# Low parts of the projection weights and of the down weights' later operands: from GpSimd to VectorE

## The chip, the cores and the metric

The kernel runs on one core of a Trainium2 chip. The metric is device time in microseconds (us) of one execution: TensorE multiplies matrices, VectorE, ScalarE and GpSimd work elementwise, SyncE issues most of the transfers between HBM and the on-chip memory (SBUF). In the profile's rows PE is TensorE, PEld its weight loads, DVE VectorE, ACT ScalarE, POOL GpSimd and SP SyncE; the queue names with a q behind are the engines' sequencers.

## What is computed

One layer of a hybrid encoder on 1024 prompt tokens and 8 x 16 sample tokens (1152 in all), width 1024, in float32:

```
proj = einsum("btd,de->bte", rmsnorm(x, norm1_w), w_in)       # columns for three head groups
ya = rglru(causal_conv(xa)) * gelu(ga)                        # group A
yb = ssd_mixer(z, causal_conv(xbc), dt)                       # group B, chunked state
yc = hgrn_mixer(q, fpre, ig, og)                              # group C, chunked state
x = x + einsum("bte,ed->btd", concat(ya, yb, yc), w_out)
h2 = rmsnorm(x, norm2_w)
ff = silu(h2 @ w_ffn_gate) * (h2 @ w_ffn_up)                  # width 2816
x = x + ff @ w_ffn_down
y = rmsnorm(x, final_norm_w)
```

The outputs are y for both groups of tokens and the new states of the three head groups.

## The kernel before

Every float32 operand of a large product is split in two parts: a high part (`hi`, rounded by ScalarE to the matmul's own format) and a low part (`lo` = operand - hi). `mm3` then makes three matmuls of a product: hi x hi, hi x lo, lo x hi (lines L144, L145, L146). The low part is one subtraction of two SBUF operands, in L164 for weights that `load_w` brings in and in L180 (`split`) for everything else. This subtraction is what the change is about.

`load_w` takes a weight block of 128x1024 (two of 128x1056): a transfer into `wr_*` (two buffers), ScalarE's high part `wh_*`, the low part `wl_*` (three buffers each). The name's first letter tells the use: f, q, t, xa, ga, b for the input projection, o for the output projection (`w_out`). A counter for each of the two kinds picks the engine: of the input projection every fourth goes to VectorE (constants `WV`, `WO`), of the output projection the first alone (`XV`, `XO`), and `w_out` gives VectorE four more of its third chunk through `eng`; the rest goes to GpSimd. So of 31 input blocks 24 and of 24 output blocks 19 are on GpSimd.

The down projection works in groups of four blocks of the hidden width with a Strassen-like scheme of seven products for a pair of 2x2 blocks. `prep_a` prepares the weights of a group, for each of four column pairs `mp`: a transfer into `wd` (or, every fourth time, into the row buffer `rrow`), a first split of three operands (128x768; on VectorE, for mp 3 on GpSimd), four additions on VectorE (L1107 to L1110) that form the later four operands in place, and a second split of these (128x1024), on GpSimd. `prep_b` does the like for the activations (`e`, L1096), the larger piece on VectorE, the smaller on GpSimd. `products` runs the seven products and adds each to one or two accumulators on VectorE (L1204); `residual` adds the stored x on GpSimd (L1239, L1241). `prep_a` of the next group runs while the present one is multiplied.

Three more places matter. `proj_vdt` multiplies the nine token tiles with the t0 weights into two pairs of PSUM banks (`ptv`) and evicts them in L428 and L430 (`dtr`, `vs`); beside it `proj_f` makes 18 scans of 128x128 on VectorE (L410, `bc`), two tiles `ct` before them (L405) and two products on GpSimd (L406), and q1's tile is evicted in L311. `mix_c` prepares the C mixer's decay factors `W`: two subtractions on VectorE (L488, L489), an exponential (L490), products on VectorE and GpSimd (L498, L502), then the matmul `pat`. `mixt` loads the mixed rows through GpSimd's own queue.

The order of each engine's instructions is set when the program is built, by a list scheduler that works with modelled durations; each engine then executes in order. If an instruction changes engine, other instructions' places change too.

Of the kernel before, what the change touches and what calls it, by code (L numbers as in the profile page):

```python
# [51 lines left out]
WV = 4  # L52
# [12 lines left out]
WO = 0  # L65
XV = 100
XO = 1
# [23 lines left out]
def hybrid_step(ctx, tc, xT, xTp, vec, rows, nrow, wch, wtk0, wtk1, wout, wgate, wup, wdown,  # L91
# [3 lines left out]
    V, S, G, T = nc.vector, nc.scalar, nc.gpsimd, nc.tensor  # L95
# [52 lines left out]
    def feed():  # L148
        return tc.high_priority(offset=PRI)

    wcount, pcount, bcount = [0, 0], [0, 0], [0]

    def load_w(src, n, name, raw=None, ahead=True, eng=None):
        if raw is None:
            raw = wp.tile([P, 1056], F32, tag="wraw", name=f"wr_{name}", bufs=2)
        hi = wp.tile([P, 1056], F32R, tag="whi", name=f"wh_{name}")
        lo = wp.tile([P, 1056], F32R, tag="wlo", name=f"wl_{name}")
        with feed() if ahead else nullcontext():
            dma(raw[:, 0:n], src)
            S.activation(hi[:, 0:n], raw[:, 0:n], AF.Copy)  # L160
            o = name[0] == "o"
            wcount[o] += 1
            e = V if wcount[o] % (WV, XV)[o] == (WO, XO)[o] else G
            (eng or e).tensor_tensor(lo[:, 0:n], raw[:, 0:n], hi[:, 0:n].bitcast(F32), ALU.subtract)  # L164
        return hi, lo

# [11 lines left out]
    def split(dst_hi, dst_lo, src, eng):  # L178
        S.activation(dst_hi, src, AF.Copy)  # L179
        eng.tensor_tensor(dst_lo, src, dst_hi.bitcast(F32), ALU.subtract)  # L180
# [80 lines left out]
    def ch_tile(m, name):  # L261
        w = load_w(wch[m], 1024, name)
        for c in range(NCHUNK):
            hT = st["hT", c]
            tg = "a"
            if name[0] in "fq":
                tg = "aabbccc"[pcount[0] % 7]
                pcount[0] += 1
            pm = bank(tg, f"pm{name}_{c}", [CH])
            for k in range(KD):  # L270
                mm3(pm, wk(w, k, P), (hT[:, 0, k, :], hT[:, 1, k, :]), k == 0, k == KD - 1)
            yield c, pm
# [149 lines left out]
    def proj_vdt():  # L422
        w = [load_w(wtk0[h], 1056, f"t0{h}") for h in range(2)]
        for t, pm in tok_piece(w, 264, "v"):
            r = rstd1[:, t:t + 1]
            sg = pr.tile([P, 256], F32, tag="stg", name=f"vs{t}", bufs=2)
            with feed():
                V.scalar_tensor_tensor(dtr[:, t * 8:t * 8 + 8], pm[:, 0:8], r, dtb, ALU.mult, ALU.add)  # L428
                if VE:
                    V.tensor_scalar(sg, pm[:, 8:264], r, None, ALU.mult)  # L430
                else:
                    S.activation(sg, pm[:, 8:264], AF.Copy, scale=r)
                dma(vod[t, :, 0:256], sg)
# [12 lines left out]
    def proj_og():  # L446
        w = [load_w(wtk1[2, h], 1024, f"t3{h}") for h in range(2)]
        proj_gate(w, "og", vod[:, :, 256:512])
# [610 lines left out]
    def a_view(mp):  # L1059

        return AS[mp].rearrange("p (a f o s) -> p a f o s", a=2, f=2, s=P)
# [13 lines left out]
    def stage(n, name):  # L1075
        k = pcount[1] % 4
        pcount[1] += 1
        if k == 3 and n <= NTOK:
            return rrow[:, 0:n]
        if k == 1:  # L1080
            return pg.tile([P, 1280], F32, tag="xb", name=name)[:, 0:n]
        return io.tile([P, 1280], F32, tag="xTin", name=name, bufs=XB)[:, 0:n]
# [16 lines left out]
    def prep_a(g, mp):  # L1099
        t = stage(1024, f"wd{g}_{mp}")  # L1100
        v = a_view(mp)
        with feed():
            dma(t, wdown[mp, :, (2 * g - 1) * 512:(2 * g + 1) * 512])
            t = t.rearrange("p (f q s) -> p f q s", q=4, s=P)
            split(v[:, 0, :, 0:3], v[:, 1, :, 0:3], t[:, :, 0:3], G if mp in PA else V)

            V.tensor_tensor(t[:, :, 2], t[:, :, 3], t[:, :, 2], ALU.add)  # L1107
            V.tensor_tensor(t[:, :, 3], t[:, :, 0], t[:, :, 3], ALU.subtract)
            V.tensor_tensor(t[:, :, 0], t[:, :, 2], t[:, :, 0], ALU.subtract)
            V.tensor_tensor(t[:, :, 1], t[:, :, 1], t[:, :, 0], ALU.subtract)  # L1110
            split(v[:, 0, :, 3:7], v[:, 1, :, 3:7], t, G)


    acc = {}
# [174 lines left out]
    for g in range(NG):  # L1289
        final = g == NG - 1  # L1290
        for s in (1, 0):
            for mp in range(4):
                if g == 0:
                    products0(s, mp)
                    if s == 1:
                        prep_a(1, mp)
                    continue
                if final and s == 0:
                    products(g, s, mp, late)
                    for t in MID.split('/')[mp]:  # L1300
                        tokens_out(int(t))
                    continue
                products(g, s, mp)
                if not final and s == 0:
                    prep_a(g + 1, mp)
            if 0 < g < NG - 1:
                residual(s, g - 1)
            if not final:
                prep_b(g + 1, s)
# [86 lines left out]
```

## Time and profile before

| what | value |
|---|---|
| median of 3 runs | 1501.31 us (1500.36 to 1501.39) |
| the profiled execution's own time | 1499.57 us |
| its span, first to last instruction | 1497.8 us |
| TensorE busy | 1367.8 us (91%) |
| VectorE busy | 1122.1 us (75%) |
| ScalarE busy | 513.9 us (34%) |
| GpSimd busy | 792.9 us (53%) |
| mean granted TensorE clock | 0.960 |

Busy time of VectorE counts the time that an instruction stands still after it has begun. The stages in order: input projection and C mixer until about 410 us, z columns until 460, B mixer and output projection until 660, gate and up projection until 1190, down projection until 1450, final norm. TensorE is busy without a break from 750 to 1190 us; the change touches nothing there.

### The profile page before, as it was taken

What the parts mean: (1) busy time and instruction counts of PE and PEld (TensorE: products, weight loads), DVE (VectorE), ACT (ScalarE), POOL (GpSimd) and SP (SyncE); (2) the same over time, 40 slices, a digit from 0 to 9 for tenths busy, and PEclk for the clock granted to TensorE, in tenths of its full rate; (3) what the DMA queues carried; (4) which work ended last, traced back from release to release, by engine and by line L of the source; (5) the groups of instructions that cost most, each with busy time, mean ns of one, the idle gap of its engine ahead of it and who ended that gap; (6) DMA issues with size and microseconds to landing.
All of it is one profiled execution on the core that took longest, in us unless ns stands there. A gap on an engine that the chain in (4) does not pass through costs nothing. (4 is left out here: it accounts for less than half of the span.)

```text
span 1497.8 us, 24592 instructions
## 1 busy us (share of the span) xinstructions
PE 1367.8 (91%) x9309; PEld 1315.9 (88%) x9309; DVE 1122.1 (75%) x2028; ACT 513.9 (34%) x839; POOL 792.9 (53%) x615
## 2 busy tenths in 40 slices
PE   7979988899997889878799999999999999988886
PEld 6979887799987778878699999999999989988876
DVE  8476799888758688599646675665666768989896
ACT  6413334333344134354322222232231443322322
POOL 5336487767345555433534554544555464475553
PEclk9989999899999899988899999999999999999988
DMA  7253221432366786841413222223322262543523
GB/s 249 75 173 102 71 68 50 104 96 75 100 224 238 225 285 208 273 167 37 150 55 112 100 96 99 70 84 113 112 98 99 85 218 85 171 149 92 172 64 127
DMA packets 103370, 193.67 MB, mean 129 GB/s; under 512 B 10380, under 2 KB 62676, under 8 KB 103124
## 3 DMA queue, kind: packets, MB, share of 16 engines
q1 hardware_dynamic: 98356, 184.24, 37.4%
q0 software_dynamic: 4896, 7.87, 1.9%
q8 instruction: 73, 1.20, 0.3%
q14 instruction: 45, 0.37, 0.1%
HBM read 136.83 MB, written 55.23 MB: 128 GB/s over the span
## 5 line engine op out<-in xcount | busy, mean ns | idle before, releaser
L144 PE MATMUL pd<-e,as 128*128 128x320 f32 (+1 forms) x560 | 170.2, 305 | 25.4 <-DVE ac_pt L1204 9.1
L145 PE MATMUL pd<-e,as 128*128 128x320 f32 (+1 forms) x560 | 166.4, 298 | 0.8 <-DVE e L1096 0.8
L146 PE MATMUL pd<-e,as 128*128 128x320 f32 (+1 forms) x560 | 163.3, 297 | 0.6 <-POOL as L180 0.6
L144 PEld LDWEIGHTS pd<-e,as 128*128 128x128 f32 x560 | 106.8, 191 | 32.1 <-DVE ac_pt L1204 9.4
L180 POOL TENSOR_TENSOR al_u<-wr_u,ah_u 128x1024 fp32r<-128x1024 f32 x30 | 72.1, 2404 | 118.4 <-ACT ah_u L179 118.4
L180 POOL TENSOR_TENSOR al_g<-wr_g,ah_g 128x1024 fp32r<-128x1024 f32 x30 | 72.3, 2412 | 88.6 <-ACT ah_g L179 88.0
L145 PEld LDWEIGHTS pd<-e,as 128*128 128x128 f32 x560 | 107.1, 191 | 1.2 <-DVE e L1096 1.1
L146 PEld LDWEIGHTS pd<-e,as 128*128 128x128 f32 x560 | 106.5, 192 | 0.9 <-POOL as L180 0.9
L1005 POOL TENSOR_TENSOR g<-g,pt_u 128x256 f32<-128x256 f32 (+1 forms) x80 | 77.3, 985 | 22.9 <-DVE pt_u L1004 16.1
L179 ACT ACTIVATE ah_g<-wr_g 128x1024 fp32r<-128x1024 f32 x30 | 31.7, 1060 | 146.6 <-PE pS_u L145 71.8
L144 PE MATMUL pw<-mT,wh_o 128*128 128x384 f32 x192 | 69.1, 363 | 11.4 <-DVE xr L785 5.5
L498 POOL TENSOR_TENSOR qbd<-W,qkb 64x128 f32<-64x128 f32 x60 | 51.7, 861 | 48.7 <-ACT W L490 16.0
L144 PE MATMUL pS_g<-b,ah_g 128*128 128x256 f32 (+1 forms) x240 | 71.3, 298 | 5.2 <-ACT ah_g L179 5.2
L146 PE MATMUL pA_g<-b,al_g 128*128 128x256 f32 (+1 forms) x240 | 71.2, 297 | 0.5 <-POOL al_g L180 0.5
L144 PE MATMUL pA_g<-b,ah_g 128*128 128x256 f32 (+1 forms) x240 | 71.4, 298 | 0.0
L145 PE MATMUL pA_g<-b,ah_g 128*128 128x256 f32 (+1 forms) x240 | 71.0, 296 | 0.0
L145 PE MATMUL pA_u<-b,ah_u 128*128 128x256 f32 (+1 forms) x240 | 71.0, 296 | 0.0
L145 PE MATMUL pS_g<-b,ah_g 128*128 128x256 f32 (+1 forms) x240 | 71.0, 296 | 0.0
L144 PE MATMUL pA_u<-b,ah_u 128*128 128x256 f32 (+1 forms) x240 | 70.9, 295 | 0.0
L146 PE MATMUL pA_u<-b,al_u 128*128 128x256 f32 (+1 forms) x240 | 70.8, 295 | 0.0
L144 PE MATMUL pS_u<-b,ah_u 128*128 128x256 f32 (+1 forms) x240 | 70.4, 295 | 0.0
L145 PE MATMUL pS_u<-b,ah_u 128*128 128x256 f32 (+1 forms) x240 | 70.3, 295 | 0.0
(722 smaller groups left out, 5118.2 us busy)
## 6 DMA issues: line engine op xcount, KB each, us to landing
wr_o<-in_dram SPq DMA_DIRECT2D x24, 512.0 KB, 5.3
wr_g<-in_dram SPq DMA_DIRECT2D x20, 512.0 KB, 3.5
wr_u<-in_dram SPq DMA_DIRECT2D x20, 512.0 KB, 3.6
wd<-in_dram SPq DMA_DIRECT2D x15, 512.0 KB, 3.7
wr_t<-in_dram SPq DMA_DIRECT2D x14, 512.0 KB, 3.8
fr<-ffd SPq DMA_DIRECT2D x11, 640.0 KB, 4.0
ffd<-g SPq DMA_DIRECT2D x10, 640.0 KB, 3.0
ffd<-g SPq DMA_DIRECT2D x10, 512.0 KB, 2.9
```

The source lines that it names most:

```text
L144: T.matmul(out, ah, bh, start=start, stop=False)
L145: T.matmul(out, ah, bl, start=False, stop=False)
L146: T.matmul(out, al, bh, start=False, stop=stop)
L179: S.activation(dst_hi, src, AF.Copy)
L180: eng.tensor_tensor(dst_lo, src, dst_hi.bitcast(F32), ALU.subtract)
L498: (V, G)[r].tensor_tensor(Q[rs, l - lg, :, r, :].rearrange("p j (b m) -> p j b m", m=m), W[rs, l - lg].rearrange("p j (b two m) -> p j b t ...
L1005: G.tensor_tensor(g, g, u, ALU.mult)
```

## The change

All subtractions of `load_w` for which no engine is given go to VectorE, and so does the second split of `prep_a`.

```diff
             o = name[0] == "o"
             wcount[o] += 1
-            e = V if wcount[o] % (WV, XV)[o] == (WO, XO)[o] else G
+            e = V
             (eng or e).tensor_tensor(lo[:, 0:n], raw[:, 0:n], hi[:, 0:n].bitcast(F32), ALU.subtract)
...
             V.tensor_tensor(t[:, :, 1], t[:, :, 1], t[:, :, 0], ALU.subtract)
-            split(v[:, 0, :, 3:7], v[:, 1, :, 3:7], t, G)
+            split(v[:, 0, :, 3:7], v[:, 1, :, 3:7], t, V)
```

On GpSimd, in the down projection, one `prep_a` of group 3 stood before like this (`as0` to `as3` are the operands of the four `mp`, `128x2x512` is a second split, `e` is from `prep_b`, `xr`, `rrow` and `ac` from `residual`):

```order
L1096 TENSOR_TENSOR e1_11655<-fr3114_12813,e1_11655 128x960
L180 TENSOR_TENSOR as0_11657<-rrow_87,as0_11657 128x2x512
L180 TENSOR_TENSOR as3_11660<-wd3_3_13074,as3_11660 128x2x384
L180 TENSOR_TENSOR as1_11658<-wd3_1_12940,as1_11658 128x2x512
L1239 TENSOR_TENSOR rrow_87<-rrow_87 128x256
L1241 TENSOR_TENSOR ac_g0_11685<-ac_g0_11685,rrow_87 128x256
```

The second splits have left it; only mp 3's first split stays.

On VectorE the same place of the changed kernel (`pd2_...` are the products of the group before, `ac_...` the accumulators):

```order
L1110 TENSOR_TENSOR rrow_87<-rrow_87 128x2x128
L1204 TENSOR_TENSOR ac_pt01_11688<-ac_pt01_11688,pd2_024_12983 128x256
L1204 TENSOR_TENSOR ac_pt02_11689<-ac_pt02_11689,pd2_022_12991 128x256
L1108 TENSOR_TENSOR wd3_1_12940<-wd3_1_12940 128x2x128
L1204 TENSOR_TENSOR ac_g1_11686<-ac_g1_11686,pd2_021_12999 128x256
L1204 TENSOR_TENSOR ac_pt10_11690<-ac_pt10_11690,pd2_030_13017 128x256
L1204 TENSOR_TENSOR ac_pt11_11691<-ac_pt11_11691,pd2_030_13017 128x256
L180 TENSOR_TENSOR as2_11659<-wd3_2_13007,as2_11659 128x2x384
L1109 TENSOR_TENSOR wd3_1_12940<-wd3_1_12940 128x2x128
L180 TENSOR_TENSOR as0_11657<-rrow_87,as0_11657 128x2x512
L1204 TENSOR_TENSOR ac_pt12_11692<-ac_pt12_11692,pd2_036_13034 128x256
```

The last split but one row is the moved one, of mp 0; it follows mp 0's last addition (the first row) with eight rows between, and accumulator additions stand behind it. Before, the same rows stood there without it.

On VectorE, around the t0 tiles in the first 100 us (- is the order before, + the change; `wl_t30` is a moved low part, `ptv_0` the first t0 tile):

```order
-L405 SCALAR_TENSOR_TENSOR ct1_548<-f1_311,ct1_548 128x1152
+L164 TENSOR_TENSOR wl_t30_953<-wr_t30_951,wh_t30_952 128x1024
+L428 SCALAR_TENSOR_TENSOR dtr_307<-ptv_0_690,rstd1_86,rw_93 128x8
+L430 TENSOR_SCALAR vs0_715<-ptv_0_690,rstd1_86 128x256
 L410 SCALAR_TENSOR_TENSOR bc0_558<-cm_91,ct0_547 128x128
 L410 SCALAR_TENSOR_TENSOR bc0_558<-cio_80,ct0_547 128x128 x8
+L405 SCALAR_TENSOR_TENSOR ct1_548<-f1_311,ct1_548 128x1152
+L428 SCALAR_TENSOR_TENSOR dtr_307<-ptv_2_748,rstd1_86,rw_93 128x8
 L410 SCALAR_TENSOR_TENSOR bc1_573<-cm_91,ct1_548 128x128
-L410 SCALAR_TENSOR_TENSOR bc1_573<-cio_80,ct1_548 128x128 x8
-L428 SCALAR_TENSOR_TENSOR dtr_307<-ptv_0_690,rstd1_86,rw_93 128x8
-L430 TENSOR_SCALAR vs0_715<-ptv_0_690,rstd1_86 128x256
```

The eviction of the first t0 tile stood behind all 18 scans and stands before them now, right behind the moved low part; the eviction of q1 (L311), next in either order, now comes after the tenth scan, ahead of the last eight.

## Rows read from the trace of the kernel before

**Rows 1.** Busy time by stretch: length, then PE, PEld, DVE, ACT, POOL, PEclk, DMA share
```profile
85.30:89.30 4.00, 3.94 (x18) 3.97 (x19) 2.80 (x5) 2.22 (x2) 0.04 (x1) 0.50 0.91 250
100.00:460.00 360.00, 334.10 (x2192) 311.38 (x2191) 291.66 (x613) 139.15 (x244) 224.56 (x229) 0.96 0.35 108
460.00:660.00 200.00, 173.49 (x961) 160.88 (x960) 156.44 (x249) 73.67 (x138) 107.06 (x77) 0.91 0.72 230
1250.00:1450.00 200.00, 176.59 (x1255) 170.53 (x1253) 183.77 (x328) 57.40 (x62) 118.04 (x78) 0.97 0.41 128
```
**Rows 2.** TensorE's groups, 1190 to 1450 us: busy us, mean ns, idle before, releasers
```profile
L144 PE MATMUL pd<-e,as 128*128 128x320 f32 (+1 forms) x496 | 150.9, 306 | 24.4 <-DVE ac_pt L1204 9.1 <-DVE ac_whi L1204 6.9 <-DVE ac_g L1204 3.0
```
**Rows 3.** One line, L164: count, then shortest/median/longest in ns
```profile
L164 POOL TENSOR_TENSOR wl_o<-wr_o,wh_o x19: 2356/2387/3260, 484.2 to 646.0; 128x1024 fp32r<-128x1024 f32 x19
...
L164 DVE TENSOR_TENSOR wl_o<-wr_o,wh_o x5: 1212/1219/2810, 468.9 to 654.6; 128x1024 fp32r<-128x1024 f32 x5
```
**Rows 4.** Timeline of GpSimd, then VectorE, 1315 to 1324 us: start, length
```profile
1316.12 2.39 POOL L180 TENSOR_TENSOR as<-wd,as 128x1024 fp32r<-128x1024 f32 x1 [3.45 <-ACT as L179]
1318.47 0.92 POOL L1239 TENSOR_TENSOR rrow<-rrow 128x256 f32<-128x256 f32 x1
1319.35 2.48 POOL L1241 TENSOR_TENSOR ac_g<-ac_g,rrow 128x256 f32<-128x256 f32 x3
1321.79 2.58 POOL L180 TENSOR_TENSOR as<-wd,as 128x1024 fp32r<-128x1024 f32 x1
...
1315.54 0.41 DVE L1108 TENSOR_TENSOR wd<-wd 128x256 f32<-128x256 f32 x1
...
1316.67 2.13 DVE L1109 TENSOR_TENSOR wd<-wd 128x256 f32<-128x256 f32 x1
1318.72 0.95 DVE L1107 TENSOR_TENSOR wd<-wd 128x256 f32<-128x256 f32 x1
...
1321.26 0.85 DVE L1108 TENSOR_TENSOR wd<-wd 128x256 f32<-128x256 f32 x1
...
1322.83 1.83 DVE L1109 TENSOR_TENSOR wd<-wd 128x256 f32<-128x256 f32 x1
```
**Rows 5.** VectorE's groups, 1190 to 1450 us, shapes kept apart
```profile
L1096 DVE TENSOR_TENSOR e<-fr,e 128x1024 fp32r<-128x1024 f32 x10 | 19.4, 1949 | 7.0 <-ACT e L1093 7.0
L1109 DVE TENSOR_TENSOR wd<-wd 128x256 f32<-128x256 f32 x15 | 18.2, 1213 | 0.0
...
L180 DVE TENSOR_TENSOR as<-wd,as 128x768 fp32r<-128x768 f32 x9 | 14.0, 1560 | 1.6 <-ACT as L179 1.6
L1108 DVE TENSOR_TENSOR wd<-wd 128x256 f32<-128x256 f32 x15 | 11.8, 786 | 0.0
...
L1107 DVE TENSOR_TENSOR wd<-wd 128x256 f32<-128x256 f32 x15 | 9.3, 623 | 0.0
L180 DVE TENSOR_TENSOR as<-rrow,as 128x768 fp32r<-128x768 f32 x4 | 8.3, 2063 | 0.9 <-ACT as L179 0.9
```
**Rows 6.** Whom TensorE waited for: us in total, times, longest
```profile
PE pat L139 <- POOL W L502: 10.3, 6, 4.5
PE ptv L144 <- DVE vs L430: 9.6, 1, 9.6
```
**Rows 7.** Timeline of GpSimd, then VectorE, at 264 us
```profile
264.67 2.46 POOL L164 TENSOR_TENSOR wl_b<-wr_b,wh_b 128x1024 fp32r<-128x1024 f32 x1
...
264.57 0.28 DVE L488 TENSOR_TENSOR W<-qkb 128x128 f32<-128x128 f32 x1
264.77 2.50 DVE L489 TENSOR_TENSOR W<-qkb 128x128 f32<-128x128 f32 x1
```
**Rows 8.** Timeline of GpSimd, then VectorE, 74 to 85 us
```profile
74.53 2.48 POOL L164 TENSOR_TENSOR wl_t<-wr_t,wh_t 128x1024 fp32r<-128x1024 f32 x1
...
74.77 7.10 DVE L410 TENSOR_TENSOR_SCAN bc<-cio,ct 128x128 f32<-128x128 f32 x8
...
84.75 0.47 DVE L430 TENSOR_SCALAR vs<-ptv,rstd 128x256 f32<-128x256 f32 x1
```

## The prediction

> **What bounds the kernel now.** I read the busy shares by stretch first. From 100 to 460 us VectorE is busy 291.66 of 360 us and GpSimd 224.56; from 460 to 660 us it is 156.44 of 200 against 107.06; in the down projection, from 1250 to 1450 us, 183.77 of 200 [rows 1]. The first two stretches hold the moved low parts of `load_w`, the third those of `prep_a`. What the reader is to see: in the third VectorE leaves 16 us of 200 unused, so there it sets the pace beside TensorE. The grouped lines say the same from the other side: TensorE's first matmul of a product stood idle 24.4 us in the down stretch, and the releasers named first are VectorE's accumulator additions [rows 2]. Then I read one line, L164, for the price of the same instruction on either engine: median 2387 ns on GpSimd, 1219 ns on VectorE [rows 3].
>
> The view that decides most is the timeline of both engines together. While a GpSimd split of 2.39 us runs from 1316.12, a VectorE addition that begins at 1316.67 takes 2.13 us, and its like beside it takes 0.41 [rows 4]. VectorE's instructions with two SBUF operands stand still while GpSimd's runs. So a split on GpSimd isn't free for VectorE, and the question is whether it costs VectorE more from outside than from inside.
>
> **The change, part by part.** 63 instructions of 128x1024 change engine: 43 in `load_w` (24 of the input projection, 19 of the output projection) and 20 in `prep_a`. GpSimd loses some 63 x 2.4 = 151 us, VectorE gains 63 x 1.22 = 77 us [rows 3].
>
> *Down stage, 20 splits.* Added: 20 x 1.22 = 24.4 us. Taken away: what the old splits make VectorE wait. Lines L1107 to L1109 took 9.3 + 11.8 + 18.2 = 39.3 us for 45 instructions; unhindered 45 x 0.41 = 18.5, so 20.8 us is waiting, and 20/15 of it, 27.8, with the five groups that go through the row buffer [rows 4, 5]. The first splits (9 and 4 of 128x768) took 22.3 us against 13 x 0.92 = 12.0 (0.92 is an estimate, 768/1024 of 1.22), another 10.3. Together 38.1 us. Not all is due to the moved splits: of four late additions in the stretch shown, two wait for a moved split (1.72 + 1.42 us), two for residual work that stays (0.54 + 0.44), so I take 3.14/4.12 = 76%, 29.0 us. The new splits can themselves be held up by what GpSimd keeps: the nearest row is VectorE's other 128x1024 split, mean 1.95 us, 0.73 over its price, but it stands beside GpSimd's half of the same data, which the moved ones don't; I take 0.2 each, 4 us, between 0 and 14.6. Sum: 24.4 + 4 - 29.0 = -0.6, say **-1 us**. Ends: all 38.1 relieved and no new waiting, -13.7; half relieved and full new waiting, 24.4 + 14.6 - 19.0 = +20. VectorE executes in order, so behind each moved split stand accumulator additions, and TensorE waits for those; the order above shows them. The splits' wait for ScalarE's high part was harmless on GpSimd; the order puts eight VectorE rows between the last addition and the split, which I take to be enough for the high part.
>
> *Stretches 100 to 660 us, 38 splits.* Added 38 x 1.22 = 46.4 us. Relief per split as in the down stage, 29.0/20 = 1.45 us, times the lower share that VectorE is busy (448.1/560 = 80% against 92%): 1.26, so 48 us. VectorE's time is unchanged: **0**, between -6 and +6 for where the pieces fall in the order. GpSimd's relief, though, is clear gain where TensorE waits for it: 10.3 us for GpSimd's product with W in the C mixer [rows 6]. Ahead of one such wait a moved split from 264.67 turned a 0.28 us subtraction into 2.50 [rows 7]; the two large waits of this kind aren't both behind a moved split, so I take **-1.5 us**, between 0 and -6. Past GpSimd's queue, the loads of `mixt` are issued no later than before; I cost that at nothing, since the splits ahead of them only go away.
>
> *First 100 us, 5 splits.* The order around the t0 tiles changes. TensorE stood 9.6 us at 75 to 85 us for VectorE's eviction vs [rows 6], because that stood behind 18 scans, eight of which took 7.10 us beside GpSimd's work, a moved split from 74.53 among it [rows 8]. Afterwards the granted clock was 0.50, the lower level of 1.2 GHz, for some 4 us, which costs 2 more [rows 1]. In the new order the first eviction stands before the scans. The next thing late is the eviction of the q1 tile behind the first nine scans (some 3 us of waiting), then the C mixer's first loads, whose operands come from those scans. Of 11.6 us, 3.3 come back at once and more later; ends 0 and -11.6, I take **-5 us**.
>
> Sum: -5 - 1.5 + 0 - 1 = -7.5. The profiled execution took 1499.57 us, 1.74 below the median 1501.31, so I forecast 1492.1 in its terms and **1494 us** as a median.
>
> The Trainium skill's page SBUF — State Buffer, section Who interferes with whom, has a rule that speaks against the change: a VectorE instruction with two SBUF inputs and a GpSimd one that reads SBUF exclude each other, and whichever starts first keeps the port for its whole length. The trace agrees on one side (2.13 us for 0.41 above). By that rule each moved split would also stop GpSimd for up to 1.22 us; where GpSimd is the one waited for that could return the -1.5 us, which lies inside the bound given.
>
> **The rivals.** *No measurable change* (1498 to 1504). The waiting only changes sides: less behind GpSimd, as much on VectorE, and the early 5 us are eaten by the C mixer's chain. For it: VectorE's sums for 58 of the splits (24.4 + 4 + 46.4 = 75 added, 29 + 48 = 77 relieved) nearly cancel. Against: the 9.6 us gap has a visible cause that the new order removes. Time: 1501.3 - 1.5 = 1500. The Trainium skill's page Perfetto Trace Analysis, section Optimizing Scalar/DVE Operations, says of the shared port that moving work between these two engines might not help; that is this rival, and no row of the kernel before tells it from the forecast.
>
> *Slower.* Place: the down projection, where VectorE is 92% busy. If the relief per split falls below its price of 1.22 us, thus under 24.4 of the 38.1 us, VectorE's surplus delays the evictions and TensorE stops for banks. With half the relief and 0.4 us new waiting each: 24.4 + 8 - 19 = +13; less 5 early: 1501.3 + 8 = 1509; the bigger end, +20, would give 1516. For it: in-order VectorE, the idle row of TensorE. Against: the late additions stand right beside the moved splits in time.
>
> *Large gain* (1481 to 1486): the whole early gap and clock, 10, and two thirds of the down stage's -13.7. Against: several other waits follow each.
>
> That the change doesn't do what it says can be put aside: the order shows the 63 instructions on VectorE.
>
> **How the numbers follow.** About 0.2%, 3 us, is what a measurement can tell from no change. Forecast and large gain together 0.50 (0.44 and 0.06), no change 0.22, slower 0.28. The likeliest case alone reaches from 1484 to 1498, by halving and doubling its terms. Since both signs hold much, the range takes in the slower rival: 1481 to 1513, which leaves out some 0.15 to 0.2, the far bounds.
>
> **What would show it.** VectorE's busy time near 1122 us although it has 63 instructions more, GpSimd's near 640. L1107 to L1109 near 0.5 us each. The moved splits at 1.2 to 1.4 us. No 9.6 us wait of ptv, TensorE done with the t0 tiles some 5 us sooner. The down stage of the same length within 3 us. I am wrong if ptv's gap stays or reappears as a wait of the C mixer, if the splits take 2 us and more on VectorE, or if TensorE's idle time before pd grows beyond 24.4 us.

## The result and the profile after

The changed kernel takes **1459.61 us** (median of 4 runs, 1456.95 to 1461.40) against 1500.84 for the kernel before on the same chip: ratio 0.9725, 95% interval 0.9708 to 0.9742. That is 41 us less. I had forecast 1494, with a range from 1481 to 1513: the sign was right, the size far off, and the time lies outside the range.

The page of the changed kernel, busy time and clock over the span of 1455.2 us:

```profile
PE 1354.3 (93%) x9309; PEld 1309.0 (90%) x9309; DVE 1098.5 (75%) x2091; ACT 515.3 (35%) x839; POOL 641.4 (44%) x552
```

GpSimd lost 151.5 us and 63 instructions, as forecast. VectorE has those 63 more and is busy for 23.6 us *less* (1122.1 before); I had expected no difference. The moved instruction has the forecast price, to be set against [rows 3]:

```profile
L164 DVE TENSOR_TENSOR wl_o<-wr_o,wh_o x24: 1209/1225/3312, 450.5 to 633.3; 128x1024 fp32r<-128x1024 f32 x24
L164 DVE TENSOR_TENSOR wl_t<-wr_t,wh_t x16: 1205/1224/1259, 51.0 to 445.6; 128x1024 fp32r<-128x1024 f32 x14, 128x1056 fp32r<-128x1056 f32 x2
```

**Where the time went.** A mark is the moment at which TensorE's first or last instruction of a tile begins or ends in the trace; the profiled execution of each kernel is compared with that of the kernel before:

| mark | before, us | after, us | gain so far |
|---|---|---|---|
| last `ptv` (t0 tiles) | 108.0 | 100.8 | 7.2 |
| last `ptog` | 135.4 | 132.0 | 3.4 |
| last `po` (C mixer) | 395.4 | 391.8 | 3.6 |
| first `ptz` (z columns) | 398.8 | 387.6 | 11.2 |
| last `ptz` | 482.0 | 470.6 | 11.4 |
| last `px` (B mixer) | 591.0 | 573.3 | 17.7 |
| last `pw` (output projection) | 666.1 | 644.9 | 21.2 |
| last `pA_u` (up projection) | 1188.0 | 1164.8 | 23.2 |
| first `pt` (final norm) | 1454.1 | 1410.1 | 44.0 |

So some 18 us come between 135 and 666 us, and 21 in the down projection, which takes 245 us in place of 266. The first `ptz` comes 11.2 us sooner because the z columns now begin before the C mixer's last products; at the end of these (`po`) TensorE is 3.6 us ahead, as at 135 us. The 18 us come behind the C mixer: 8 until the last z columns, 6 until the last `px`, 3.5 until the last `pw`. Busy time of the whole down stage, before and after (columns as in [rows 1]):

```profile
1188.00:1454.00 266.00, 239.20 (x1705) 231.87 (x1704) 233.81 (x415) 86.21 (x111) 153.90 (x98) 0.97 0.42 132
```
```profile
1165.00:1410.00 245.00, 234.43 (x1703) 228.64 (x1702) 221.76 (x434) 87.00 (x111) 101.32 (x78) 0.99 0.47 144
```

VectorE has 19 recorded instructions more and 12.0 us less to do. Before the first matmul of a product TensorE now stands 7.7 us, where it stood 25.4 on the page of before [rows 2], and its releasers have changed: ScalarE's and VectorE's parts of the weights, no longer the accumulators.

```profile
L144 PE MATMUL pd<-e,as 128*128 128x256 f32 (+1 forms) x560 | 167.2, 300 | 7.7 <-ACT as L179 4.6
L146 PE MATMUL pd<-e,as 128*128 128x256 f32 (+1 forms) x560 | 162.3, 297 | 3.1 <-DVE as L180 3.1
```

VectorE's groups in the same stage, to be set against [rows 5]: L1107 to L1109 fell from 623, 786 and 1213 ns to 567, 575 and 505, L1096 of 1024 columns from 1949 to 1324 (L1110 rose from 457 to 639), and the moved splits themselves cost 18.8 + 6.4 = 25.2 us.

```profile
L180 DVE TENSOR_TENSOR as<-wd,as 128x1024 fp32r<-128x1024 f32 x15 | 18.8, 1261 | 0.0
L1096 DVE TENSOR_TENSOR e<-fr,e 128x1280 fp32r<-128x1280 f32 x10 | 15.1, 1511 | 10.4 <-ACT e L1093 10.4
L1096 DVE TENSOR_TENSOR e<-fr,e 128x1024 fp32r<-128x1024 f32 x10 | 13.2, 1324 | 2.5 <-ACT e L1093 2.5
L180 DVE TENSOR_TENSOR as<-wd,as 128x768 fp32r<-128x768 f32 x11 | 12.2, 1111 | 2.3 <-ACT as L179 2.3
L1110 DVE TENSOR_TENSOR wd<-wd 128x256 f32<-128x256 f32 x15 | 9.6, 639 | 0.0
L1108 DVE TENSOR_TENSOR wd<-wd 128x256 f32<-128x256 f32 x15 | 8.6, 575 | 0.0
L1107 DVE TENSOR_TENSOR wd<-wd 128x256 f32<-128x256 f32 x15 | 8.5, 567 | 0.0
L1109 DVE TENSOR_TENSOR wd<-wd 128x256 f32<-128x256 f32 x15 | 7.6, 505 | 0.0
L180 DVE TENSOR_TENSOR as<-rrow,as 128x1024 fp32r<-128x1024 f32 x5 | 6.4, 1275 | 0.0
```

In the B mixer one line shows it best: L744, which scales the mixer's rows before they are transposed for the output projection. Before:

```profile
L744 DVE SCALAR_TENSOR_TENSOR ws<-ws,ssb,nwr 128x256 f32<-128x256 f32 x8 | 12.7, 1632 | 2.1 <-POOL ssb L172 2.1
L744 DVE SCALAR_TENSOR_TENSOR wb<-wb,ssb,nwr 128x256 f32<-128x256 f32 x10 | 10.6, 1095 | 0.8 <-POOL ssb L172 0.8
```

and after:

```profile
L744 DVE SCALAR_TENSOR_TENSOR wb<-wb,ssb,nwr 128x256 f32<-128x256 f32 x10 | 4.5, 479 | 0.7 <-POOL ssb L172 0.7
L744 DVE SCALAR_TENSOR_TENSOR ws<-ws,ssb,nwr 128x256 f32<-128x256 f32 x8 | 3.6, 482 | 0.9 <-POOL ssb L172 0.9
```

Of the 18, seven took 2.4 to 3.2 us before, and the other eleven 0.47 or 0.48. Beside each of the seven a 2.4 us subtraction of `load_w` on GpSimd was running. TensorE's transposes (`pmb`) stood for these rows before:

```profile
PE pmb L748 <- DVE ws L744: 4.0, 2, 2.5
PE pmb L748 <- DVE wb L744: 3.3, 2, 1.8
```

After, TensorE has no wait for L744. The timeline of one pair in the kernel before (GpSimd, VectorE: start, length), and of the same pair after:

```profile
577.18 2.40 POOL L164 TENSOR_TENSOR wl_o<-wr_o,wh_o 128x1024 fp32r<-128x1024 f32 x1
...
577.24 3.01 DVE L744 SCALAR_TENSOR_TENSOR wb<-wb,ssb,nwr 128x256 f32<-128x256 f32 x2 [0.82 <-POOL ssb L172]
```
```profile
562.11 0.88 DVE L744 SCALAR_TENSOR_TENSOR wb<-wb,ssb,nwr 128x256 f32<-128x256 f32 x2 [0.36 <-POOL ssb L172]
```

A second trail is in the waits of SP's queue, which issues the loads in a fixed order. In the down stage of the kernel before, the loads of the next activations (L1090) and of the stored x (L1237) stood for GpSimd's low parts, since these had to be done with a buffer before it could be filled again:

```profile
SPq L1090 <- POOL as L180: 53.5, 11, 9.5
SPq L1237 <- POOL as L180: 35.3, 4, 10.2
```

After, the first is 22.5 us behind VectorE's low parts, and the second is gone from the longest waits:

```profile
SPq L1090 <- DVE as L180: 22.5, 9, 7.0
SPq L1103 <- POOL e L1096: 21.8, 10, 2.8
SPq L1237 <- DVE ac_whi L1204: 14.3, 1, 14.3
```

These are waits of a queue that runs ahead, so they aren't time by themselves; but they are a way for a slow low part to cost time, beside the way through VectorE.

### The profile page after: what moved, and what is told of

Read it like the earlier page. It is cut to its first block, busy times and chain, and to the rows that moved or that the text cites. A ratio compares the mean times of both kernels' runs of the same rounds, so it can differ in the third digit from the quotient of the medians.

```text
span 1455.2 us, 24583 instructions
## 1 busy us (share of the span) xinstructions
PE 1354.3 (93%) x9309; PEld 1309.0 (90%) x9309; DVE 1098.5 (75%) x2091; ACT 515.3 (35%) x839; POOL 641.4 (44%) x552
## 4 chain that ended last, share of the span: by engine, by line
PE 60%; DVE 22%; DMA 8%; issue 4%; POOL 2%; ACT 2%; SPq 0%; DVEq 0%; POOLq 0%; ACTq 0%
PE pS_g L144 3%; PE pS_g L145 3%; PE pd L144 3%; PE pS_u L144 3%; PE pS_g L146 3%; PE pS_u L145 3%; PE pS_u L146 3%; PE pd L146 3%; PE pd L145 3%; PE pA_u L144 2%; PE pA_u L146 2%; PE pA_u L145 2%; PE pA_g L145 2%; PE pA_g L144 2%; PE pA_g L146 2%
## 5 line engine op out<-in xcount | busy, mean ns | idle before, releaser
L144 PE MATMUL pd<-e,as 128*128 128x256 f32 (+1 forms) x560 | 167.2, 300 | 7.7 <-ACT as L179 4.6
L146 PE MATMUL pd<-e,as 128*128 128x256 f32 (+1 forms) x560 | 162.3, 297 | 3.1 <-DVE as L180 3.1
L145 PE MATMUL pd<-e,as 128*128 128x256 f32 (+1 forms) x560 | 164.6, 295 | 0.0
L180 POOL TENSOR_TENSOR al_u<-wr_u,ah_u 128x1024 fp32r<-128x1024 f32 x30 | 72.1, 2403 | 119.0 <-ACT ah_u L179 116.1
L180 POOL TENSOR_TENSOR al_g<-wr_g,ah_g 128x1024 fp32r<-128x1024 f32 x30 | 71.9, 2397 | 90.4 <-ACT ah_g L179 89.6
L498 POOL TENSOR_TENSOR qbd<-W,qkb 64x128 f32<-64x128 f32 x60 | 54.3, 905 | 62.5 <-ACT W L490 25.6
L144 PE MATMUL pS_u<-b,ah_u 128*128 128x256 f32 (+1 forms) x240 | 70.6, 295 | 0.0
L146 PE MATMUL pS_u<-b,al_u 128*128 128x256 f32 (+1 forms) x240 | 70.5, 294 | 0.0
```

What stands on the lines that cost most here:

```text
L144: T.matmul(out, ah, bh, start=start, stop=False)
L145: T.matmul(out, ah, bl, start=False, stop=False)
L146: T.matmul(out, al, bh, start=False, stop=stop)
L498: (V, G)[r].tensor_tensor(Q[rs, l - lg, :, r, :].rearrange("p j (b m) -> p j b m", m=m), W[rs, l - lg].rearrange("p j (b two m) -> p j b t ...
```

## The experiments

Three theories. **A**: a GpSimd subtraction holds VectorE, and the gain is there where TensorE waits for VectorE. **B**: the scheduler's other order is what gained. **C**: GpSimd's time or queue is what costs, whoever waits. Later **D**: the low part is simply ready sooner. All ratios are against the kernel before.

**1 to 4: the parts.** Each keeps one part of the change. In the first, only `load_w`:

```diff
-            split(v[:, 0, :, 3:7], v[:, 1, :, 3:7], t, V)
+            split(v[:, 0, :, 3:7], v[:, 1, :, 3:7], t, G)
```

> The 43 low parts of load_w on VectorE, the 20 of prep_a on GpSimd as before. Theory A (a GpSimd subtraction holds VectorE, and what counts is where TensorE waits for VectorE): the changed kernel was 23 us ahead of the one before at the start of the down projection and 44 us ahead at its end, so this half alone gives about -21 us (1476 to 1484 us), all of it before 1190 us, and the down stage is as long as before (266 us). Theory B (the gain is the other order of instructions, not the moved work): the halves do not add up; this one and the other half together miss -41 us by over 8 us. Theory C (what counts is GpSimd time freed, whoever waits): 43 of 63 subtractions, so -28 us (1473 us).

In the second, only `prep_a`:

```diff
-            e = V
+            e = V if wcount[o] % (WV, XV)[o] == (WO, XO)[o] else G
```

> The 20 low parts of prep_a on VectorE, the 43 of load_w as before. Theory A: about -21 us (1476 to 1484 us), all of it between the start and the end of the down projection, which takes 245 us in place of 266. Theory B: not the rest of -41 us to e1_loadw_only, off by over 8 us. Theory C: 20 of 63, so -13 us (1488 us).

The third and fourth divide `load_w` (with `prep_a` on GpSimd): `e = V if not o or ...` for the input projection, `e = V if o or ...` for the output projection.

> Only the 24 low parts of the input projections on VectorE. Theory A: the gain before 500 us is where these weights are used (t0, t1 and the first of mixer B), so this takes most of what load_w gives: -14 to -21 us (1480 to 1487 us). Theory C: 24 of 63, so -16 us (1485 us). They are told apart by the next run, not by this one.

> Only the 19 low parts of the output projection on VectorE. Theory A: between 500 and 720 us the changed kernel gained nothing and at 745 us some 3 us, so -2 to -5 us (1496 to 1499 us). Theory C: 19 of 63, so -12 us (1489 us). Theory B: any figure, and with e3_input_only not the sum that e1_loadw_only shows.

The marks are those of the one profiled execution of each kernel; for `prep_a` only and for the input part it was 4 and 6 us faster than the median.

| kernel | median, us | ratio (95%) | last `px` | last `pw` | last `pA_u` | down stage |
|---|---|---|---|---|---|---|
| before | 1500.14 | | 591.0 | 666.1 | 1188.0 | 266 |
| load_w only | 1479.41 | 0.9847 (0.9827 to 0.9866) | 573.8 | 648.2 | 1169.3 | 265 |
| prep_a only | 1483.57 | 0.9881 (0.9852 to 0.9910) | 589.6 | 662.1 | 1185.9 | 248 |
| input only | 1495.32 | 0.9964 (0.9940 to 0.9988) | 587.2 | 658.1 | 1180.3 | 264 |
| output only | 1485.95 | 0.9896 (0.9878 to 0.9914) | 579.6 | 654.8 | 1175.1 | 265 |

The halves add up: 1.53% + 1.19% = 2.72%, against 2.75% for the whole; with intervals of 3 to 4 us on each half, so close a match is in part luck. The gain of each half lies in its own stage: `load_w` leaves the down stage at 265 us, `prep_a` shortens it to 248 and leaves the rest nearly as it was. B is unlikely as the main cause, since it would have to give two independent orders that happen to add up; that some us of each half come from the other order isn't excluded. C's figures (28 and 13 us) were missed too: measured 23 and 18.

My division of `load_w` was wrong. The output projection's 19 gave 15.6 us (I had expected 2 to 5) and the input projection's 24 gave 5.4 (expected 14 to 21). The trace tells why: the weights of the output projection are prepared ahead, beside the B mixer, and there they hold VectorE's small instructions, L744 among them, not those of the output projection. With the output part alone TensorE is level at the first `px` (421.0 in both) and 11.4 us ahead at the last. With the input part alone it is 10.6 us ahead at the first `px` (410.4) and only 3.8 at the last; with the other 19 moved too, the lead grows from 10.8 to 17.2.

**5 and 6: a useless GpSimd instruction in the down stage.** The changed kernel, with one line more behind `prep_a`'s split; the operand `t` isn't read after it:

```diff
+            G.tensor_tensor(t, t, v[:, 0, :, 3:7].bitcast(F32), ALU.subtract)
```

> The changed kernel, with a useless GpSimd subtraction of the same size (operand and high part read, the result written over the operand, which nobody reads again) behind each of prep_a's 20 VectorE subtractions. No low part comes later for it; GpSimd has its load of before, and its two reads. Theory A (a GpSimd subtraction holds VectorE): the down stage goes back from 245 towards 266 us, so 1472 to 1482 us in place of 1460. Theory D (what gained was that the low part is ready 1.2 us sooner, on VectorE): no change, 1457 to 1463 us.

or with two memsets of the same tile in its place:

```diff
+            for _ in range(2):
+                G.memset(t, 0.0)
```

> As e5_ghost_reads, but with two memsets of the operand in place of the subtraction: about 2 x 1.05 = 2.1 us of GpSimd each time (0.52 us for 512 columns in the trace of before), without a read. Theory A in its narrow form (it is GpSimd's reads that hold VectorE): 1458 to 1465 us. Theory C (GpSimd's queue or its load is what costs): the same as e5_ghost_reads, 1472 to 1482 us.

Measured: 1492.73 us (0.9951, 0.9934 to 0.9968) with the subtraction, 1471.48 (0.9814, 0.9793 to 0.9834) with the memsets. Against 0.9725 that is 34 and 13 us; the down stage takes 281 and 254 us in place of 245. A had allowed 12 to 22 and up to 5. C had forecast 1472 to 1482 us for both, and they lie 21 us apart. The low parts are made by VectorE in both, so D alone doesn't explain the gain. The down stage with the subtraction and with the memsets, to be set against the changed kernel's above:

```profile
1165.00:1446.00 281.00, 247.66 (x1701) 238.95 (x1700) 254.07 (x432) 87.61 (x112) 159.81 (x99) 0.95 0.40 125
```
```profile
1168.00:1422.00 254.00, 233.58 (x1694) 228.04 (x1693) 222.35 (x428) 86.72 (x111) 143.38 (x118) 0.99 0.44 139
```

With the subtraction TensorE stood 33 us in the stage where it had stood 11, and it was busy 13 us longer, at a granted clock of 0.95 in place of 0.99. VectorE's rows with the subtraction, beside GpSimd's; L1205 is the accumulator addition, one line lower than before:

```profile
L1112 POOL TENSOR_TENSOR wd<-wd,as 128x1024 f32<-128x1024 f32 x15 | 40.8, 2727 | 21.0 <-DVE as L180 21.0
...
L180 DVE TENSOR_TENSOR as<-wd,as 128x1024 fp32r<-128x1024 f32 (+1 forms) x26 | 38.8, 1500 | 3.9 <-ACT as L179 3.9
L1096 DVE TENSOR_TENSOR e<-fr,e 128x1280 fp32r<-128x1280 f32 (+1 forms) x20 | 34.2, 1713 | 14.5 <-ACT e L1093 14.5
L1205 DVE TENSOR_TENSOR ac_whi<-ac_whi,pd 128x320 f32<-128x320 f32 x62 | 27.3, 474 | 2.1 <-PE pd L146 2.0
L180 DVE TENSOR_TENSOR as<-rrow,as 128x1024 fp32r<-128x1024 f32 (+1 forms) x9 | 15.5, 1720 | 0.2 <-ACT as L179 0.2
```

and with the memsets:

```profile
L1113 POOL MEMSET wd<- 128x1024 f32 x30 | 28.4, 956 | 18.9 <-DVE as L180 18.4
...
L180 DVE TENSOR_TENSOR as<-wd,as 128x1024 fp32r<-128x1024 f32 (+1 forms) x26 | 34.4, 1325 | 4.8 <-ACT as L179 4.6
L1096 DVE TENSOR_TENSOR e<-fr,e 128x1280 fp32r<-128x1280 f32 (+1 forms) x20 | 30.3, 1514 | 20.5 <-ACT e L1093 20.5
```

Beside the subtraction VectorE's instructions with two SBUF operands (L180 from `wd`, and L1096, both forms together) grew from 1198 to 1500 and from 1418 to 1713 ns; the accumulator addition, one of whose operands lies in PSUM, stayed at 474. VectorE's busy time in the stage rose from 222 to 254 us, with the memsets only to 222.4. In the memset kernel the two means grew as well, to 1325 and 1514, but not beside the memsets: of the rows of L180, L1096 and L1107 to L1110, 21 ran beside a memset and no other GpSimd instruction, and each took what its like took beside none (128x256 additions 409 to 417 ns, 128x1024 subtractions 1209 to 1216). The long ones all ran beside a GpSimd instruction that reads SBUF. So GpSimd's subtraction holds VectorE and its writing doesn't, which is A in its narrow form. The 13 us that the memsets cost all the same are beyond A's range and just below C's. The added instructions also changed the order of the others (on VectorE at least 220 of 2091 stand elsewhere with the subtraction, 249 with the memsets), so neither time is that of the added work alone.

**7 and 8: the same behind `load_w`'s 43 subtractions**, on the raw weight:

```diff
+            if eng is None and wcount[o] % (WV, XV)[o] != (WO, XO)[o]:
+                G.tensor_tensor(raw[:, 0:n], raw[:, 0:n], hi[:, 0:n].bitcast(F32), ALU.subtract)
```

> The changed kernel, with the same useless GpSimd subtraction behind load_w's VectorE subtraction, for the 43 weights whose low part GpSimd made before. Theory A: most of load_w's 23 us comes back, above all between 410 and 650 us, so 1474 to 1485 us. Theory D: 1457 to 1464 us.

> As e7_ghost_loadw with two memsets of the raw weight, 2.1 us without a read. Theory A in its narrow form: 1458 to 1467 us. Theory C: the same as e7_ghost_loadw. A wait for the raw weight's buffer, which both hold some 2 us longer, would show in both.

Measured: 1516.45 us (1.0113, 1.0093 to 1.0133), slower than the kernel before, and 1482.53 (0.9887, 0.9858 to 0.9916) with memsets. Both are beyond what A allowed them, by 31 and 16 us, and in the same pattern: the memsets cost 23 us, and the subtraction 34 us more than that. TensorE was 51 us behind the changed kernel at the last `px` with the one, 14 with the other. With the memsets 12 us more were lost between the last `pw` and the last `pA_u`, behind the last of these weights; I didn't find why.

**9: more of the same.** If GpSimd's subtractions cost so much, nine more of them go to VectorE:

```diff
-PA = (3,)
+PA = ()
...
-            split(b_part(s, k, 0, 0, 3), b_part(s, k, 1, 0, 3), t[:, 0:3, :], (V, G)[k % 2])
+            split(b_part(s, k, 0, 0, 3), b_part(s, k, 1, 0, 3), t[:, 0:3, :], V)
```

> The changed kernel, with two more groups of GpSimd subtractions on VectorE: the first low part of each down weight whose mp is 3 (5 in all, 2.06 us on GpSimd in the trace after) and two of the four first low parts of each of build's two calls (4 in all, 2.2 to 2.4 us). Theory A: VectorE pays about 1 us for each and is held less; TensorE waits only 10.8 us in the down stage of the changed kernel, so -1 to -4 us in all (1455.5 to 1458.5 us). Rival: VectorE, at 222 of 245 us, is now what TensorE waits for, and each of the 9 costs about 1 us: +5 to +9 us (1465 to 1469 us).

Measured: 1465.79 us (0.9779, 0.9757 to 0.9801), 8 us slower than the changed kernel by the ratios. The time is the rival's: the down stage went from 245 to 252 us, where TensorE's waits for the accumulator additions grew from 2.5 to 7.5 us and those for ScalarE's high parts from 4.6 to 7.1, and the gate projection's first products ended 5 us later. VectorE's busy time in the stage hardly changed (222 and 223 us): what the moved subtractions added was about what was relieved.

**10, 14 and 15: the buffer, the order, or the reads.** A memset of 8 columns of the operand, which holds its buffer with next to no work for GpSimd; the same on a dead tile `n2`, meant as the same instruction without the buffer; and half the useless subtraction:

```diff
+            G.memset(t[:, 1, 3, 0:8], 0.0)
```

> The changed kernel with one GpSimd memset of 8 columns of the operand (0.1 us) behind each of prep_a's 20 VectorE subtractions. The operand's buffer is held until GpSimd has come to it, as in e5_ghost_reads and e6_ghost_writes, but GpSimd has next to no work for it. If the 12 us of e6_ghost_writes are the holding of the buffer and the turn in GpSimd's queue, this has most of them: 1466 to 1472 us. If they are GpSimd's 2 us of writing, or the other order of the instructions: 1458 to 1463 us.

```diff
+            G.memset(n2, 0.0)
```

> As e10_touch, but the 0.1 us memset goes to eight columns of a scale that nobody reads any more (n2), so that the operand's buffer is not held for it. If the 11 to 12 us of e10_touch and e6_ghost_writes are the holding of the buffer until GpSimd has come to it: 1458 to 1463 us. If any added instruction moves the others so that the time goes up: 1466 to 1472 us.

```diff
+            G.tensor_tensor(t[:, 1], t[:, 1], v[:, 0, 1, 3:7].bitcast(F32), ALU.subtract)
```

> As e5_ghost_reads, with half the columns (512 of 1024) in the useless GpSimd subtraction. The buffer is held as in e10_touch (1471 us). If each column that GpSimd reads holds VectorE, the time lies half way between e10_touch and e5_ghost_reads (1492 us): 1478 to 1486 us. If it is the instruction and not its reads: 1468 to 1474 us.

| written behind each of the 20 splits | median, us | ratio (95%) | down stage, us |
|---|---|---|---|
| nothing (the changed kernel) | 1459.61 | 0.9725 (0.9708 to 0.9742) | 245 |
| 8 columns of a dead tile (ran before the stage) | 1462.95 | 0.9760 (0.9739 to 0.9781) | 247 |
| 8 columns of the operand | 1470.98 | 0.9813 (0.9790 to 0.9837) | 259 |
| two memsets of the operand | 1471.48 | 0.9814 (0.9793 to 0.9834) | 254 |
| half the subtraction | 1475.10 | 0.9844 (0.9827 to 0.9860) | 260 |
| the whole subtraction | 1492.73 | 0.9951 (0.9934 to 0.9968) | 281 |

The kernel with the dead tile isn't the comparison that I meant it to be. Nothing ties its memsets to the splits, and the scheduler put all 20 far ahead of the stage; those on the operand ran behind their splits (first and last start in us):

```profile
L1112 POOL MEMSET vc<- x20: 94/104/137, 662.8 to 668.2; 128x8 f32 x20
...
L1112 POOL MEMSET wd<- x15: 95/104/112, 1181.2 to 1417.3; 128x8 f32 x15
```

All its other instructions stand in the order of the changed kernel, on every engine. So its 5 us by the ratios, 2 in the down stage, are no price of another order: they show how far two measurements of the same order can lie apart. (Of the 7.9 us between the two profiled executions 5.3 had been lost at the last `pw`, before the first memset.)

The 8 columns of the operand cost 13 us, by the ratios and in the down stage alike. They hold the buffer until GpSimd has come by, and they changed the order as well: on VectorE at least 59 of 2091 instructions stand elsewhere. How much is the one and how much the other isn't shown. That two memsets of the whole operand cost no more speaks against the time that GpSimd works. In the trace of the 8 columns SP's queue stands for GpSimd again:

```profile
SPq L1090 <- POOL wd L1112: 22.4, 10, 5.1
...
SPq L1238 <- POOL rrow L1112: 13.8, 2, 9.2
SPq L1238 <- POOL wd L1112: 13.2, 4, 8.7
```

The half subtraction cost 5 us more than the touch by the ratios, 1 in the down stage of the profiled executions, and so lies between my two ranges, where I had put 10; the whole one cost 21. The cost isn't in proportion to what GpSimd reads. VectorE is busy 230.6, 235.2 and 254.1 us in the three. The stage with the half subtraction, to be set against that with the whole one above:

```profile
1165.00:1424.00 259.00, 237.74 (x1702) 229.07 (x1701) 235.17 (x430) 88.41 (x112) 131.58 (x98) 0.99 0.44 137
```

Of the 22 us between them 10 are TensorE's busy time, at a granted clock of 0.99 and 0.95, and 12 its idle time. Why the second half brings so much more waiting I didn't settle.

**11 and 12: the C mixer.** There GpSimd's product of keys and weights (L502) is what TensorE waits for longest in the changed kernel, and GpSimd reads there 120 times beside VectorE:

```diff
-                G.tensor_tensor(w0, w0, halves(kk, m)[0], ALU.mult)
+                V.tensor_tensor(w0, w0, halves(kk, m)[0], ALU.mult)
```

> The changed kernel, with the C mixer's 60 products of keys and weights (L502, 865 ns each on GpSimd) on VectorE, where the neighbouring products of 128x128 (L488, L489) take 0.30 to 0.39 us: VectorE pays 15 to 20 us between 100 and 410 us, where it is busy 250 of 310 us. Theory A: VectorE is held less by GpSimd's reads (its excess over its shortest durations is 40 us there), and TensorE's 8.4 us of waiting for L502 go: -3 to -8 us (1452 to 1457 us). Rival: VectorE is the engine that TensorE waits for there, and pays more than it is relieved: 0 to +8 us (1460 to 1468 us).

> As e11_keys_on_vector, and the 60 products of queries that GpSimd makes (L498, 905 ns) on VectorE too (412 ns there): GpSimd reads nothing in that loop any more. Theory A: VectorE pays 15 us more than in e11_keys_on_vector (60 x 0.25 us undisturbed) and is relieved of most of the rest: -2 to -8 us (1452 to 1458 us). Rival: +5 to +15 us (1465 to 1475 us).

In the second, `(V, G)[r]` of L498 is `V` too. Measured: 1461.18 us (0.9745, 0.9724 to 0.9765), no difference from the changed kernel that these runs can tell, and 1465.90 (0.9771, 0.9745 to 0.9797), some 7 us slower by the ratios. Both lie in the rival's range. In the first the wait for L502 went from 8.4 to 1.7 us, and VectorE's busy time from 236.3 of 285 us to 254.9 of 290:

```profile
100.00:385.00 285.00, 265.21 (x1659) 245.73 (x1659) 236.27 (x531) 106.74 (x181) 178.16 (x200) 0.96 0.27 83
```
```profile
100.00:390.00 290.00, 275.38 (x1739) 254.36 (x1737) 254.94 (x605) 112.22 (x189) 131.65 (x141) 0.96 0.28 86
```

No kernel of this study beats the changed one.

## Why the prediction was wrong

**The mechanism was right.** VectorE's instructions with two SBUF operands stand still while GpSimd's subtraction runs [rows 4, 7]; experiments 5 and 6 show it by itself. The Trainium skill's page SBUF — State Buffer, section Who interferes with whom, says that a VectorE instruction with two SBUF inputs contends with a GpSimd instruction that reads SBUF, and not with one that only writes it. These traces agree on both sides: beside the useless subtraction L1096 grew from 1418 to 1713 ns, while beside the memsets alone such rows kept their time. The price of a moved split was right as well (1.22 forecast; medians of 1.20 to 1.23 measured in L164, a mean of 1.26 in the down stage), and so was GpSimd's busy time (640 forecast, 641.4).

**The first 100 us: -5, right.** The t0 tiles were done 7.2 us sooner, and 3.4 of it lasted. The eviction in the new order stands before the scans, the 9.6 us wait [rows 6] is gone, and what came next is what I had named, q1's tile:

```profile
PE ptv L144 <- DVE q L311: 3.8, 1, 3.8
```

The granted clock was at its lower level, 0.50, from 79.5 to 89.7 us before [rows 1] and is there from 80.7 to 84.1 now, after a wait of 3.8 us in place of 9.6; in the stretch of [rows 1] TensorE now works without a break at the full level:

```profile
85.30:89.30 4.00, 4.00 (x35) 4.00 (x34) 2.66 (x6) 0.00 (x0) 0.24 (x2) 1.00 0.75 238
```

**The down stage: -1, measured -21.** Two things failed.

- *The relief was mis-sized.* Of the lines I counted, L1107 to L1109 went from 52.1 to 33.3 us and the first splits from 24.3 to 17.1, 26.0 together, close to the 29.0 I took. But I left out L1096, whose 1949 ns stood in the very rows I used [rows 5]; I took it as held by GpSimd's half of the same data, which stays. It gave 8.3 us (36.6 to 28.3). VectorE's whole busy time in the stage fell by 12.0 us after 25.2 had been added: 37.2 were relieved, not 29.0. And the 4 us of new waiting for the moved splits were 0.8 (25.2 against 20 x 1.22).
- *One path was left out.* I priced the change on VectorE alone. The operand's buffer too was held until GpSimd was done with it, and the loads behind it on SP's queue stood for that, 53.5 and 35.3 us. Experiments 6 and 10, in which VectorE makes the low parts but the buffers wait for GpSimd, took 9 and 13 us more in this stage, with an order of their own. How the 21 us divide between the two paths isn't shown. TensorE's idle time fell by some 16 us, and its busy time by 4.8, at a granted clock of 0.99 after 0.97.

**100 to 660 us: 0 and -1.5, measured some -18.** Until the end of the C mixer the two terms held: the lead is 3.6 us there, as at 135 us. The wait for L502 fell from 10.3 to 8.4 us, near the -1.5, and that for the eviction of L505 rose from 3.9 to 10.2. The 18 us came behind it, and here the step that failed is the balance itself: "VectorE's time is unchanged: 0". As a total it was not far off in the second half: from 410 to 666 us VectorE was busy 194.2 us before, and from 399 to 645 it is 191.2.

```profile
410.00:666.00 256.00, 221.98 (x1331) 207.15 (x1330) 194.24 (x321) 102.06 (x192) 127.96 (x89) 0.93 0.72 232
```
```profile
399.00:645.00 246.00, 219.55 (x1378) 209.88 (x1378) 191.16 (x350) 103.99 (x194) 63.01 (x63) 0.95 0.74 244
```

But the stretch became 10 us shorter. VectorE is idle for over 50 us there, so a total says little. What was added, subtractions of weights that are needed much later, can fall into that idle time; what was relieved are short instructions in a serial chain, like L744, some 2 us late when it met a subtraction, with TensorE's transposes behind it. TensorE's 7.3 us of waiting for L744 are gone; the rest of the gain here I haven't followed line by line. I had even scaled the relief *down* because VectorE is less busy there (1.26 us for 1.45). Over the whole stretch it was larger: VectorE's time from 100 to 666 us fell from 453.8 to 436.7 us (to 645) with 38 x 1.22 = 46.4 us added, so 63.5/38 = 1.67 us each.

**The rivals.** *No change* rested on VectorE's sums nearly cancelling. They did so in one stretch, and the time fell there all the same. The Trainium skill's page Perfetto Trace Analysis, section Optimizing Scalar/DVE Operations, says that moving work between these two engines might not help. Here, from GpSimd to VectorE, it took 2.75% off the time. *Slower* needed less relief than the price of 1.22 us; it was 37.2/20 = 1.86 in the down stage. *Large gain* had the right direction, but I gave it 0.06 and let it end at 1481, since I bounded the relief by the lines that I had added up and the early gap, and gave the middle stretch nothing. With the middle at its measured 18 and the down stage at its lower bound of -13.7 the same sum would have come to 5 + 18 + 14 = 37.

## What to carry to other kernels

Where GpSimd's work with SBUF operands holds VectorE, this case says not to weigh the move by VectorE's total: list the VectorE instructions that are on TensorE's path, see how many of them ran beside the GpSimd one, and charge the added work only where VectorE has no idle time. Count every group whose mean lies above its shortest duration, and look at the buffers that the slow engine holds and the queue that waits to fill them; what these are worth isn't shown here. Look again after the move: with VectorE at 222 of 245 us, nine more such moves already cost 8 us. And when an instruction is added as a test, look up in the trace where it ran and whether the others kept their order.

## What I had not expected

- An 8-column memset on GpSimd, 20 times 0.1 us of work, cost 11 us (1470.98 against 1459.61), through the buffer that it holds, the order that it changes, or both.
- The same memsets on a dead tile were executed some 500 us ahead of the splits behind which they are written.
- GpSimd's useless subtraction took 2727 ns where its split of the same size had taken 2513 in this stage, and half of it cost 5 us over the touch, the whole 21.
- The output projection's weights do their harm in the B mixer, a stage before the one that uses them.
